# Output projection of a hybrid encoder step: prompt tokens in 2x2 blocks with seven products instead of eight

## The chip, the cores and the metric

The kernel runs on one core of one Trainium2 chip. The metric is device time in microseconds (us), from the start to the end of one execution, as a median of several runs. All data are float32. TensorE is called PE, VectorE DVE, ScalarE ACT, GpSimd POOL, and SyncE, which only issues transfers here, SP.

## The reference, cut to what matters

One layer of an encoder trunk is computed for 512 prompt tokens and 8 x 16 sample tokens (640 in all), with D_MODEL = 2048. Three gated attention branches are merged, and one output projection with an RMS norm and a residual follows. Only the last line is touched by the change:

```python
merged = (sigmoid(mg_sb) * branch(o_sb, g_sb, w_up_sb)
          + sigmoid(mg_bd) * branch(o_bd, g_bd, w_up_band)
          + sigmoid(mg_mm) * branch(o_mm, g_mm, w_up_mem))
return x + rms_norm(merged @ w_out, g_post)      # (640, 2048) @ (2048, 2048)
```

## The kernel before, in words

Float32 products are made of three matmuls. Every operand is split into a high part (a cast on ACT, `split`, L119) and a low part (the difference to the high part, on DVE, L120), and `mm3` (L175 to L178) adds high x high, high x low and low x high in a PSUM bank. The two parts of a weight tile are called `wh` and `wl`, those of `merged` `gh` and `gl`.

The instructions' order on each engine is fixed when the program is built; a scheduler that simulates the program places each instruction, and each engine then runs its own list in order and waits at the semaphores of its operands. What stands in a list before a waiting instruction's successor therefore counts.

Most of the span is the input projection. It already works on 2x2 blocks with seven products (`block_pair`, L746 to L808): POOL adds and subtracts weight blocks (L753, L800), ACT and DVE split the results, PE multiplies (L760). Then come attention heads with the rest of the gates between them, and the up projections (`up_steps`, L895): for each of the 16 blocks of 128 channels j, PE fills `acc`, DVE multiplies with the gate (L909), POOL adds into `merged[:, j]` (L910).

The output projection (L947 to L1029) is the part that the change replaces. `merged` has channels on the partitions, in 16 blocks of 128 (index k), and 640 tokens along a row. All 16 blocks are split when they are ready. Then four column blocks `cb` of 512 output columns follow one another, each with five PSUM banks `ya`, one for 128 tokens: for k in steps of two, SP loads a weight slab of 512 KB (`wr`, a ring of three buffers), ACT and DVE split it into `wh` and `wl` (rings of four), and PE runs 5 x 2 x 3 = 30 matmuls of 512 columns. At the end of a column block ACT takes the sums of squares (`square`, L986) and DVE scales by the gain into `yt` (`scale`, L989).

In the last column block the second half of k is kept in four slabs of their own, and the token blocks are finished one by one (4, 0, 1, 2, 3): 24 matmuls, `scale`, `square`, a chain of small operations for the norm's factor (L1019 to L1023), four multiply-adds with the residual `xres` (L1025), and the stores. So the last PE work of a token block lies under the closing work of the one before.

Of the kernel before, what the change touches and what calls it, by code (L numbers as in the profile page):

```python
# [32 lines left out]


B = dict(wr=3, wh=4, wl=4, kc=2, kt=4, vc=8, b=2, e=2, raw=1, q=1, k=1, v=1, wt=1)
LATE = 4

BESIDE = 24
PACE = 8
FIRST = 4  # L40
# [8 lines left out]
def stream_step_kernel(  # L49
# [57 lines left out]
    def rows_of(prompt, sample, t):  # L107
        return prompt[t * P:(t + 1) * P] if t < 4 else sample
# [9 lines left out]
    def split(hi, lo, src):  # L118
        ACT.copy(hi, src)  # L119
        DVE.tensor_tensor(lo, src, hi.bitcast(F32), op=ALU.subtract)  # L120
# [54 lines left out]
    def mm3(out, ah, al, bh, bl, start, stop):  # L175
        PE.matmul(out, ah, bh, start=start, stop=False)  # L176
        PE.matmul(out, ah, bl, start=False, stop=False)  # L177
        PE.matmul(out, al, bh, start=False, stop=stop)  # L178
# [687 lines left out]
    def fill_steps(done):  # L866
        for i in gates[-BESIDE:]:
            yield from gate_steps(i)

        xs.close()  # L870
        pm = br.enter_context(tc.tile_pool(name="mraw", bufs=1, side="right", reuse_waits="tile"))
# [94 lines left out]
    yt = [py.tile([P, D], F32, name=f"yt{t}") for t in range(5)]  # L966
    ssq = py.tile([P, 5, 4], F32, name="ssq")
    part = py.tile([P, 5], F32, name="part")
    for cb in range(4):
        cs = slice(cb * 512, (cb + 1) * 512)  # L970
        accs = [ps_y.tile([P, 512], F32, tag="ya", name="ya") for _ in range(5)]

        def w_slab(k0, *where):
            return load_w(w_o[k0 * P:(k0 + 2) * P, cs].rearrange("(k p) c -> p k c", p=P), [P, 2, 512], *where)

        def mm(t, k0, wh, wl):
            c = slice(t * P, (t + 1) * P)
            for kk in range(2):
                k = k0 + kk
                gh, gl = (g[:, c] for g in gparts[k])  # L980
                mm3(accs[t], gh, gl, wh[:, kk], wl[:, kk], k == 0, k == KB - 1)

        def square(t):

            sq = py.tile([P, 512], F32, tag="sq2", name="sq2", bufs=1)
            ACT.activation(sq, accs[t], AF.Square, scale=D ** -0.5, accum_out=ssq[:, t, cb:cb + 1])  # L986

        def scale(t):
            DVE.tensor_tensor(yt[t][:, cs], accs[t], gpb[:, cs], op=ALU.mult)  # L989

        late = 0 if cb < 3 else LATE
# [4 lines left out]
        if not late:  # L996
            for t in range(5):
                square(t)
                scale(t)
            continue  # L1000
        early.close()
        px = ctx.enter_context(tc.tile_pool(name="px", bufs=1, reuse_waits="tile"))
        slabs = [(k0, *w_slab(k0, py, 2 * LATE)) for k0 in range(KB - 2 * late, KB, 2)]
        xres = []
        for t in (4, 0, 1, 2, 3):
            x = px.tile([P, D], F32, name=f"xres{t}")
            SP.dma_start(x, rows_of(x_p, x_s, t))
            xres.append(x)
            DVE.tensor_reduce(part[:, t:t + 1], ssq[:, t, 0:3], op=ALU.add, axis=AX.X)
            DVE.tensor_scalar(part[:, t:t + 1], part[:, t:t + 1], EPS, None, op0=ALU.add)  # L1010
        for t, x in zip((4, 0, 1, 2, 3), xres):
            for sl in slabs:
                mm(t, *sl)
            scale(t)
            square(t)

            n = py.tile([P, 4], F32, tag="n", name="n", bufs=2)
            v, s_, r, q = (n[:, i:i + 1] for i in range(4))
            DVE.tensor_tensor(v, ssq[:, t, 3:4], part[:, t:t + 1], op=ALU.add)  # L1019
            ACT.activation(s_, v, AF.Sqrt)  # L1020
            DVE.reciprocal(r, s_)
            DVE.scalar_tensor_tensor(q, r, r, v, op0=ALU.mult, op1=ALU.mult)
            DVE.scalar_tensor_tensor(q, q, -3.0, r, op0=ALU.add, op1=ALU.mult)  # L1023
            for c in (slice(n * 512, (n + 1) * 512) for n in range(4)):
                DVE.scalar_tensor_tensor(yt[t][:, c], yt[t][:, c], q, x[:, c], op0=ALU.mult, op1=ALU.add)  # L1025
# [30 lines left out]
```

## Time and profile before

| what | value |
|---|---|
| time, median of 3 runs | 2049.0 us (2047.3 to 2050.6) |
| profiled execution: span from first to last instruction | 2044.4 us |
| what the median has beyond that span | 4.6 us |
| PE busy | 2014.2 us, 99% |
| DVE, ACT, POOL busy | 1178.5, 839.1, 705.8 us |
| chain that ended last | PE 91%, DMA 3%, DVE 2% |
| output projection | from 1816.9 us to the end |

The span belongs to one profiled execution; times of runs are a few us longer than a span because they hold what lies around it. In a row of a group, the numbers behind the bar are the total busy time in us, the mean time of one instruction in ns, and the idle time of its engine just before, with what ended it. In a row of the timeline the first two numbers are the start and the length in us. The records of PE show a matmul longer than the distance to the next one, since matmuls are pipelined.

### The profile page before, as it was taken

The page shows a single profiled execution, that of the slowest core. Times are in us where ns is not written, and L with a number is a line of the kernel's source. Part 1 is how long each engine was busy: PE and PEld are TensorE (multiplying, and loading weights), DVE is VectorE, ACT ScalarE, POOL GpSimd, SP SyncE. Part 2 cuts the span into 40 slices and gives each one's busy share as a digit, 9 for nine tenths or more (in the row PEclk, how much of TensorE's full clock was granted, in tenths as well). Part 3 has the DMA queues.
Part 4 walks back from the last instruction along what each step waited for, and adds up shares of the span by engine and source line. Part 5 has one row for each costly group of instructions (what it writes and reads, how often), then busy time and mean ns, then how long its engine had stood idle before and what let it go on. Part 6 is the DMA issues. An engine that isn't in the chain of part 4 may idle for free.

```text
span 2044.4 us, 35948 instructions
## 1 busy us (share of the span) xinstructions
PE 2014.2 (99%) x13829; PEld 1908.3 (93%) x13829; DVE 1178.5 (58%) x1830; ACT 839.1 (41%) x1577; POOL 705.8 (35%) x685
## 2 busy tenths in 40 slices
PE   8999999999999999999999999999999999999998
PEld 5999999999999999999998899999998899998886
DVE  6875577655676655555555555555556675442234
ACT  6544444444444444444443444444444332322221
POOL 1145566665666665644431011011010024330000
PEclk9999999999999999999999999999999999999999
DMA  7656676665686564663338777677679876532225
GB/s 269 218 140 150 169 207 142 168 168 149 161 205 154 137 156 130 150 150 111 118 106 280 224 221 219 214 225 225 211 214 283 255 234 178 144 123 83 73 93 216
DMA packets 548185, 361.38 MB, mean 177 GB/s; under 512 B 249169, under 2 KB 493409, under 8 KB 546477
## 3 DMA queue, kind: packets, MB, share of 16 engines
q1 hardware_dynamic: 528414, 305.80, 53.5%
q0 software_dynamic: 12688, 37.57, 5.5%
q10 hardware_dynamic: 6912, 15.73, 2.1%
q8 instruction: 108, 1.77, 0.4%
q14 instruction: 63, 0.52, 0.1%
HBM read 303.17 MB, written 90.77 MB: 193 GB/s over the span
## 4 chain that ended last, share of the span: by engine, by line
PE 91%; DMA 3%; DVE 2%; issue 1%; ACT 1%; POOL 1%; SPq 0%; ACTq 0%; DVEq 0%; POOLq 0%
PE q L760 44%; PE acc L191 27%; PE ya L176 4%; PE ya L178 4%; PE ya L177 4%; PE s L549 2%; PE o L608 1%; DMA or<-osg_d 1%; DVE wl L120 1%; PE tp L451 1%; PE acc L178 1%; PE acc L176 1%; PE acc L177 1%; PE o L177 1%; PE o L178 0%
## 5 line engine op out<-in xcount | busy, mean ns | idle before, releaser
L120 DVE TENSOR_TENSOR wl<-wr,wh 128x512 fp32r<-128x512 f32 (+1 forms) x516 | 411.7, 803 | 301.0 <-ACT wh L119 298.0
L119 ACT CAST wh<-wr 128x512 fp32r<-128x512 f32 (+1 forms) x516 | 311.7, 608 | 564.3 <-PE q L760 214.8
L120 DVE TENSOR_TENSOR wl<-ws,wh 128x512 fp32r<-128x512 f32 x304 | 285.1, 943 | 235.8 <-ACT wh L119 230.0
L760 PE MATMUL q<-xh,wl 128*128 128x320 f32 x1216 | 375.8, 309 | 0.3 <-DVE wl L120 0.3
L760 PE MATMUL q<-xh,wh 128*128 128x320 f32 x1216 | 375.7, 309 | 0.0
L760 PE MATMUL q<-xl,wh 128*128 128x320 f32 x1216 | 375.6, 309 | 0.0
L119 ACT CAST wh<-ws 128x512 fp32r<-128x512 f32 x304 | 188.1, 621 | 291.4 <-PE q L760 236.6
L760 PE MATMUL q<-th,wh 128*128 128x320 f32 x912 | 282.2, 309 | 2.0 <-ACT sig L777 2.0
L760 PE MATMUL q<-th,wl 128*128 128x320 f32 x912 | 281.9, 309 | 0.0
L760 PE MATMUL q<-tl,wh 128*128 128x320 f32 x912 | 281.8, 309 | 0.0
L760 PEld LDWEIGHTS q<-xh,wl 128*128 128x128 f32 x1216 | 228.7, 188 | 0.5 <-DVE wl L120 0.5
L760 PEld LDWEIGHTS q<-xl,wh 128*128 128x128 f32 x1216 | 228.6, 188 | 0.0
L760 PEld LDWEIGHTS q<-xh,wh 128*128 128x128 f32 x1216 | 228.5, 188 | 0.0
L191 PE MATMUL acc<-xh,wh 128*128 128x320 f32 x896 | 210.8, 313 | 0.0
L191 PE MATMUL acc<-xl,wh 128*128 128x320 f32 x896 | 209.5, 311 | 0.0
L191 PE MATMUL acc<-xh,wl 128*128 128x320 f32 x896 | 207.4, 310 | 0.0
L753 POOL TENSOR_TENSOR ws<-wr 128x512 f32<-128x512 f32 x114 | 169.1, 1496 | 81.2 <-DVE wl L120 68.5
L760 PEld LDWEIGHTS q<-th,wh 128*128 128x128 f32 x912 | 171.2, 188 | 2.7 <-ACT sig L777 2.5
L760 PEld LDWEIGHTS q<-th,wl 128*128 128x128 f32 x912 | 171.2, 188 | 0.2 <-DVE wl L120 0.2
L760 PEld LDWEIGHTS q<-tl,wh 128*128 128x128 f32 x912 | 171.2, 188 | 0.0
L191 PEld LDWEIGHTS acc<-xh,wh 128*128 128x128 f32 x896 | 150.1, 188 | 18.9 <-issue 18.4
L191 PEld LDWEIGHTS acc<-xl,wh 128*128 128x128 f32 x896 | 151.2, 188 | 0.6 <-issue 0.4
(228 smaller groups left out, 3353.1 us busy)
## 6 DMA issues: line engine op xcount, KB each, us to landing
wr<-in_w_in_dram SPq DMA_DIRECT2D x208, 512.0 KB, 4.9
kc<-keys_d SPq DMA_DIRECT2D x48, 512.0 KB, 5.8
wr<-in_w_out_dram SPq DMA_DIRECT2D x32, 512.0 KB, 3.7
sig_d<-sig ACTq DMA_DIRECT2D x48, 320.0 KB, 5.1
sig<-sig_d SPq DMA_DIRECT2D x48, 320.0 KB, 3.6
keys_d<-in_cache_sb_k_dram SPq DMA_DIRECT2D x96, 128.0 KB, 4.7
keys_d<-in_cache_band_k_dram SPq DMA_DIRECT2D x96, 128.0 KB, 4.5
vc<-in_cache_sb_v_dram SPq DMA_DIRECT2D x48, 256.0 KB, 5.6
```

The costliest lines, as they stand in the source:

```text
L119: ACT.copy(hi, src)
L120: DVE.tensor_tensor(lo, src, hi.bitcast(F32), op=ALU.subtract)
L176: PE.matmul(out, ah, bh, start=start, stop=False)
L177: PE.matmul(out, ah, bl, start=False, stop=False)
L178: PE.matmul(out, al, bh, start=False, stop=stop)
L191: PE.matmul(acc[:, s, :HF], a[:, k], b[s], start=first and f, stop=last and l)
L451: PE.transpose(tp[:, kb * P:(kb + 1) * P], b[:, kb * P:(kb + 1) * P], ident)
L549: return PE.matmul(s[32 * j:32 * j + 32, :nc_], qm[:, j, par * 32:par * 32 + 32], kts[j], start=par == 0, stop=par == 1, tile_position=(0, ...
L608: PE.matmul(o[32 * j:32 * j + 32, :P], l, r, start=i == 0, stop=i == len(steps) - 1, tile_position=(0, 32 * j))
L753: eng.tensor_tensor(o, a[c], b[c], op=op)
L760: PE.matmul(bank_, a[:, k], b[:, k], start=first and k == 0 and n == 0, stop=k == KH - 1 and n == 2, skip_group_check=not first)
```

## The change

The 512 prompt tokens are cut into two halves of 256, the 2048 inner channels k into two halves of 8 blocks, and the 2048 output columns into four parts of 512: g = 0, 1 each with a left and a right part. For each g the prompt part is a 2x2 block product, and it is computed with seven block products in place of eight. A11 to A22 are the quarters of `merged` (first index the half of the tokens, second the half of k), W11 to W22 those of the weights of one g. With S = A21+A22 and T = S-A11 the row operands are A11, S, T, A12, A12-T, A22-T and A22; with U = W12-W11 and V = W22-U the weight operands that they meet are W11, U, V, W21, W22, W22-W12 and W21-V. The 128 sample tokens are not blocked: they are multiplied plainly by four of the weight operands (W11, U, W21, W22), which is enough since the product with W11 is used for the left and the right part.

The work runs product by product, each for both g. In the text the stages are counted thus:

| stage | row operand, weight operand | matmuls |
|---|---|---|
| 1 | g1 = A11, W11; samples too | 144 |
| 2 | g5 = S, `tw` = U; samples too | 144 |
| 3 | g6 = T, `tw` = V | 96 |
| 4 | g2 = A12, W21; samples too | 144 |
| 5 | g3 = A12-T, W22, samples too (18 matmuls a step), and g7 = A22-T, W22-W12 (12 a step) | 240 |
| 6 | g4 = A22, `tw` = W21-V | 96 |

There are 864 matmuls of 512 columns in place of 960, and 112 weight tiles of 128x512 to be split in place of 64. The differences of weights are formed on POOL in tiles of 128x1024 (32 of them; L1047, L1064, L1097, L1115 of the changed kernel), two of the operands need two loaded slabs, and the loads of `w_out` are 48 of 512 KB in place of 32. Row operands live in two buffers that are used in turn, so each can be split only when the one two before it is done. Of the eight PSUM banks four (`ya`) hold sums over several products, two (`cc`) a product for a pair of token blocks, two (`cs`) the samples'. Finished parts are added into `yt` by DVE (L1028), squared by ACT and scaled by the gain on POOL (L1021). The residual is loaded into the place of `merged`. The up projection's blocks are made in the order 0, 8, 1, 9, ... so that the sums of the quarters can be formed early; otherwise everything ahead of the output projection stands in the same order as before on every engine.

The diff, cut to its core:

```diff
-    for j in range(KB):
-        split(*gparts[j], merged[:, j])
...
-    for cb in range(4):
-        cs = slice(cb * 512, (cb + 1) * 512)
-        accs = [ps_y.tile([P, 512], F32, tag="ya", name="ya") for _ in range(5)]
...
-        for k0 in range(0, KB - 2 * late, 2):
-            wh, wl = w_slab(k0)
-            for t in range(5):
-                mm(t, k0, wh, wl)
...
+    for g in range(2):
...
+        for k in range(0, KH, 2):
+            r = slab(0, g, 0, k)
+            with tc.issue_after(behind):
+                SP.dma_start(tw[g][:, k:k + 2], w_at(0, g, 1, k))
+            p = cut(r)
+            POOL.tensor_tensor(tw[g][:, k:k + 2], tw[g][:, k:k + 2], r, op=ALU.subtract)
+            for i in range(2):
+                times(ya[g][i], g1h, g1l, tok[i], k, p, True, True)
+            times(s, sh, sl, everything, k, p, True, True)
...
+    g7 = rows(a11)
+    for g in range(2):
+        s, cc = one_bank(), pair_banks()
+
+        def third(k):
+            r = slab(1, g, 1, k)
+            q = slab(0, g, 1, k)
+            p = cut(r)
+            POOL.tensor_tensor(q, r, q, op=ALU.subtract)
+            times(s, sh, sl, everything, KH + k, p, True, True)
+            for i in range(2):
+                times(cc[i], *g3, tok[i], k, p, True, True)
+            return q
+
+        q = third(0)
+        for k in range(0, KH, 2):
+            p = cut(q)
+            if k + 2 < KH:
+                q = third(k + 2)
+            into(g, *g7, k, p)
+        for i in range(2):
+            add(i, at(g, 1), cc[i])
+        add(4, at(g, 1), s)
+        for i in range(2):
+            add(2 + i, at(g, 1), ya[g][i])
+        for i in (0, 1, 4, 2, 3):
+            done_at(i, at(g, 1))
...
+    g4 = rows(a22)
...
+    for k in range(0, KH, 2):
+        into(0, *g4, k, cut(tw[0][:, k:k + 2]))
+    for i in range(2):
+        square(2 + i, at(0, 0), ya[0][i])
+        scale(2 + i, at(0, 0), ya[0][i])
...
+    slabs = [(k, cut(tw[1][:, k:k + 2], *((pl, 4) if k >= 4 else ()))) for k in range(0, KH, 2)]
+    for t in (4, 0, 1):
+        finish(t)
+    for i in range(2):
+        for k, p in slabs:
+            into(1, *g4, k, p, (i,))
+        scale(2 + i, at(1, 0), ya[1][i])
+        square(2 + i, at(1, 0), ya[1][i])
+        finish(2 + i)
```

`slab` loads 512 KB into the ring `wr` (three buffers as before), `cut` splits two tiles of 128x512 into `wh` and `wl`, `rows` splits a row operand in four tiles of 128x512, `times` and `into` issue the matmuls of one step of two k, and `finish` is the chain of the norm with the four multiply-adds and the stores.

Where the instructions stand. First DVE at the end. Before, each of the last token blocks has this list to itself (`yt_20765` and `yt_20766` are token blocks 2 and 3):

```order
L989 TENSOR_TENSOR yt_20765<-ya,gpb 128x512
L1019 TENSOR_TENSOR n<-ssq,part 128x1
L1021 RECIPROCAL n<-n 128x1
L1022 SCALAR_TENSOR_TENSOR n<-n 128x1
L1023 SCALAR_TENSOR_TENSOR n<-n 128x1
L1025 SCALAR_TENSOR_TENSOR yt_20765<-yt_20765,n,xres_22011 128x512 x4
L989 TENSOR_TENSOR yt_20766<-ya,gpb 128x512
```

Now the beginning of stage 6 reads thus on DVE (`yt_20801`, `yt_20797` to `yt_20800` are token blocks 4 and 0 to 3; `ya_20806` and `ya_20807` are the banks of g = 1):

```order
L118 TENSOR_TENSOR wl<-tw,wh 128x512
L1028 TENSOR_TENSOR yt_20801<-cs,yt_20801 128x512
L1028 TENSOR_TENSOR yt_20797<-cc,yt_20797 128x512
L1028 TENSOR_TENSOR yt_20798<-cc,yt_20798 128x512
L118 TENSOR_TENSOR gl<-merged,gh 128x512 x4
L1028 TENSOR_TENSOR yt_20799<-ya_20806,yt_20799 128x512
L118 TENSOR_TENSOR wl<-tw,wh 128x512
L1028 TENSOR_TENSOR yt_20800<-ya_20807,yt_20800 128x512
```

Between the first and the second weight tile of the stage stand four adds of stage 5's results and the four tiles of the row operand. Further down, in the middle of stage 6, DVE has:

```order
L1149 SCALAR_TENSOR_TENSOR yt_20797<-yt_20797,n,merged 128x512 x4
L1139 TENSOR_TENSOR n<-ssq,part 128x1
L118 TENSOR_TENSOR wl<-tw,wh 128x512 x7
L1141 RECIPROCAL n<-n 128x1
L1021 TENSOR_TENSOR yt_20799<-ya_20804,gpb 128x512
L1156 TENSOR_TENSOR part<-ssq 128x1
L1021 TENSOR_TENSOR yt_20800<-ya_20805,gpb 128x512
L1156 TENSOR_TENSOR part<-ssq 128x1
L1142 SCALAR_TENSOR_TENSOR n<-n 128x1
L118 TENSOR_TENSOR wl<-tw,wh 128x512
```

The four multiply-adds of token block 0 have moved ahead of the last eight weight tiles, and the last tile of all (the second k of the second step) stands behind two scalings.

On POOL the whole output projection had one instruction (the last additions into `merged` stand ahead of it, the store of the samples behind it):

```order
L910 TENSOR_TENSOR merged<-merged,sig 128x640 x21
L965 TENSOR_SCALAR gpb<-gpb 128x2048
L1029 DMA out_dram<-yt_20767 128x2048
```

Now it has, from stage 5's third to its eighth and last difference of weights:

```order
L1115 TENSOR_TENSOR wr<-wr 128x1024 x3
L1021 TENSOR_TENSOR yt_20797<-yt_20797,gpb 128x512
L1021 TENSOR_TENSOR yt_20798<-yt_20798,gpb 128x512
L1021 TENSOR_TENSOR yt_20801<-yt_20801,gpb 128x512
L1021 TENSOR_TENSOR yt_20799<-yt_20799,gpb 128x512
L1115 TENSOR_TENSOR wr<-wr 128x1024
L1021 TENSOR_TENSOR yt_20800<-yt_20800,gpb 128x512
L1115 TENSOR_TENSOR wr<-wr 128x1024 x2
```

Four scalings of finished results stand between the fifth and the sixth of the stage's eight differences, and a fifth scaling between the sixth and the last two.

More of the change, by code (lines that the diff above doesn't have):

```diff
@@ L35 @@
 B = dict(wr=3, wh=4, wl=4, kc=2, kt=4, vc=8, b=2, e=2, raw=1, q=1, k=1, v=1, wt=1)
-LATE = 4
 BESIDE = 24
@@ new lines, in w_at, with slab, cut, at @@
+    def w_at(half, g, right, k):
+        c = (2 * g + right) * C
+        r = (half * KH + k) * P
+        return w_o[r:r + 2 * P, c:c + C].rearrange("(k p) c -> p k c", p=P)
+    def slab(half, g, right, k):
+        t = pw.tile([P, 2, C], F32, tag="wr", name="wr", bufs=B["wr"])
+        SP.dma_start(t, w_at(half, g, right, k))
+        return t
+    def cut(t, *where):
+        return parts_of([t[:, n:n + 1] for n in range(2)], *where)
+    def at(g, right):
+        return slice((2 * g + right) * C, (2 * g + right + 1) * C)
@@ new lines, in times, with square @@
+    def times(acc, gh, gl, c, k0, parts, first, last):
+        wh, wl = parts
+        for n in range(2):
+            k = k0 + n
+            mm3(acc, gh[:, k, c], gl[:, k, c], wh[:, n], wl[:, n], first and k % KH == 0, last and k % KH == KH - 1)
+    tok = [slice(i * P, (i + 1) * P) for i in range(2)]
+    everything = slice(0, P)
+    def square(t, cs, src):
+        sq = stg.tile([P, NT], F32, tag="sig", name="sq")
+        n = cs.start // C
+        ACT.activation(sq[:, :C], src, AF.Square, scale=D ** -0.5, accum_out=ssq[:, t, n:n + 1])
@@ new lines, in scale, with done_at, add, pair_banks @@
+    def scale(t, cs, src, eng=DVE):
+        eng.tensor_tensor(yt[t][:, cs], src, gpb[:, cs], op=ALU.mult)
+    def done_at(t, cs, eng=POOL):
+        square(t, cs, yt[t][:, cs])
+        scale(t, cs, yt[t][:, cs], eng)
+    def add(t, cs, src, other=None):
+        DVE.tensor_tensor(yt[t][:, cs], src, yt[t][:, cs] if other is None else other, op=ALU.add)
+    ya = [[ps_y.tile([P, C], F32, name=f"ya{g}{i}") for i in range(2)] for g in range(2)]
+    def pair_banks():
+        return [ps_y.tile([P, C], F32, tag="cc", name="cc", bufs=2) for _ in range(2)]
@@ new lines, in one_bank @@
+    def one_bank():
+        return ps_y.tile([P, C], F32, tag="cs", name="cs", bufs=2)
+    for g in range(2):
+        cs1, cs2 = at(g, 0), at(g, 1)
+        s = one_bank()
+        for k in range(0, KH, 2):
[8 more added lines that the diff above has]
+        for i in range(2):
+            ACT.copy(yt[i][:, cs1], ya[g][i])
+        for c in (cs1, cs2):
+            ACT.copy(yt[4][:, c], s)
@@ new lines, in stream_step_kernel @@
+    rowsum(a21, a21, a11, ALU.subtract)
+    g6 = rows(a21)
+    for g in range(2):
+        cs1, cs2 = at(g, 0), at(g, 1)
+        s, cc = one_bank(), pair_banks()
+        for k in range(0, KH, 2):
+            p = cut(tw[g][:, k:k + 2])
+            r = slab(1, g, 1, k)
+            POOL.tensor_tensor(tw[g][:, k:k + 2], r, tw[g][:, k:k + 2], op=ALU.subtract)
+            times(s, sh, sl, everything, k, p, True, True)
+            for i in range(2):
+                times(cc[i], g5h, g5l, tok[i], k, p, True, True)
+        for i in range(2):
+            ACT.copy(yt[2 + i][:, cs2], cc[i])
+        add(4, cs2, s)
@@ new lines, in into @@
+    def into(g, gh, gl, k, p, which=(0, 1)):
+        wh, wl = p
+        for i in which:
+            for n in range(2):
+                a, b = gh[:, k + n, tok[i]], gl[:, k + n, tok[i]]
+                for l, r in ((a, wh), (a, wl), (b, wh)):
+                    PE.matmul(ya[g][i], l, r[:, n], start=False, stop=k + n == KH - 1 and r is wh and l is b,
+                              skip_group_check=True)
+    for g in range(2):
+        for k in range(0, KH, 2):
+            into(g, *g6, k, cut(tw[g][:, k:k + 2]))
+        for i in range(2):
+            add(i, at(g, 1), ya[g][i], yt[2 + i][:, at(g, 1)])
@@ new lines, in stream_step_kernel @@
+    g2 = rows(a12)
+    rowsum(a11, a22, a21, ALU.subtract)
+    rowsum(a21, a12, a21, ALU.subtract)
+    g3 = rows(a21)
+    for g in range(2):
+        s, cc = one_bank(), pair_banks()
+        for k in range(0, KH, 2):
+            r = slab(1, g, 0, k)
+            p = cut(r)
+            POOL.tensor_tensor(tw[g][:, k:k + 2], r, tw[g][:, k:k + 2], op=ALU.subtract)
+            times(s, sh, sl, everything, KH + k, p, True, True)
+            for i in range(2):
+                times(cc[i], *g2, tok[i], k, p, True, True)
+        for i in range(2):
+            add(i, at(g, 0), cc[i])
+        add(4, at(g, 0), s)
+        for i in (0, 1, 4):
+            done_at(i, at(g, 0))
```

123 lines of the change are left out of this document (67 added, 56 removed).

## Prediction

> **What bounds the kernel now.** I read the page's busy times and its chain first, then the busy times by stretches, then the groups of the output projection.
>
> ```profile
> span 2044.4 us, 35948 instructions
> PE 2014.2 (99%) x13829; PEld 1908.3 (93%) x13829; DVE 1178.5 (58%) x1830; ACT 839.1 (41%) x1577; POOL 705.8 (35%) x685
> PE 91%; DMA 3%; DVE 2%; issue 1%; ACT 1%; POOL 1%; SPq 0%; ACTq 0%; DVEq 0%; POOLq 0%
> 500.00:600.00 100.00, 100.00 (x683) 99.91 (x682) 65.38 (x75) 40.18 (x74) 63.96 (x64) 1.00 0.72 184
> 1850.00:2000.00 150.00, 150.00 (x663) 124.24 (x662) 45.72 (x77) 41.36 (x82) 0.00 (x0) 1.00 0.27 90
> 1816.00:2036.00 220.00, 218.58 (x960) 180.11 (x960) 13.61 (x20) 13.06 (x38) 1.00 0.33 114
> ```
>
> The last three rows are stretches: length, then busy time and count on PE, weight load, DVE, ACT and POOL, granted clock, DMA share. PE never rests: neither in a stretch of the input projection, which already works with seven products (POOL 64% and DVE 65% busy beside it), nor in the output projection, where DVE and ACT are below a third and POOL does nothing. So a matmul less counts in full, as long as the other engines keep up. The third stretch holds the 960 matmuls into `ya` alone: 218.58 / 960 = 0.2277 us each.
>
> **The change part by part.** 960 - 864 = 96 matmuls go: 96 x 0.2277 = 21.9 us off the path. That the change does not do this is excluded by its list of instructions. Everything else is a question of cover. The prices:
>
> ```profile
> L120 DVE TENSOR_TENSOR wl<-wr,wh 128x512 fp32r<-128x512 f32 x62 | 41.9, 691 | 119.3 <-ACT wh L119 119.3
> L119 ACT CAST wh<-wr 128x512 fp32r<-128x512 f32 x62 | 37.8, 622 | 124.2 <-PE ya L178 111.2 <-DMA wr<-in_w_out_dram 11.0 <-PE acc L191 0.9
> L986 ACT ACTIVATE sq<-ya 128x512 f32<-128x512 f32 x20 | 12.0, 599 | 40.3 <-DVE yt L989 31.5 <-PE ya L178 8.4
> L986 ACT ACTIVATION_READ_ACCUMULATOR sq<-ya 128x1 f32 x20 | 3.9, 194 | 0.0
> L965 POOL TENSOR_SCALAR gpb<-gpb 128x2048 f32<-128x2048 f32 x1 | 5.4, 5404 | 7.3 <-issue 7.3
> wr<-in_w_out_dram SPq DMA_DIRECT2D x32, 512.0 KB, 3.7
> wr<-in_w_in_dram SPq DMA_DIRECT2D x208, 512.0 KB, 4.9
> 511.71 1.28 POOL L800 TENSOR_TENSOR ws<-wr,ws 128x512 f32<-128x512 f32 x1 [0.63 <-DVE wl L120]
> 516.27 1.75 POOL L753 TENSOR_TENSOR ws<-wr,wr 128x512 f32<-128x512 f32 x1
> 522.35 3.00 POOL L753 TENSOR_TENSOR ws<-wr 128x512 f32<-128x512 f32 x2 [0.63 <-DVE wl L120]
> 523.05 1.14 DVE L120 TENSOR_TENSOR wl<-wr,wh 128x512 fp32r<-128x512 f32 x1 [0.78 <-ACT wh L119]
> 524.31 0.49 DVE L770 TENSOR_TENSOR sig<-sig,q 128x320 f32<-128x320 f32 x1
> 526.57 0.69 DVE L120 TENSOR_TENSOR wl<-wr,wh 128x512 fp32r<-128x512 f32 x1 [0.67 <-ACT wh L119]
> 527.83 0.49 DVE L770 TENSOR_TENSOR sig<-sig,q 128x320 f32<-128x320 f32 x1 [0.56 <-PE q L760]
> ```
>
> A low part costs DVE 0.69 us with POOL at rest, and 1.14 beside a running POOL operation; POOL's 128x512 costs 1.28 to 1.75. A 128x1024 difference is not in this trace: I take twice a 128x512 one, 2.6 to 3.5 us, and 2.7 where DVE has little to do. A DVE operation that reads PSUM (L770) takes 0.49 beside POOL and without it, so the adds from PSUM are not slowed.
>
> *Stages 1 to 4 (528 matmuls).* Stage 1's weights pass a ring of three slabs, and a slab is now freed only when POOL has subtracted it. POOL's last addition into `merged` comes first:
>
> ```profile
> 1816.88 0.40 PE L176 MATMUL ya<-wh,gh 128*128 128x512 f32 x1
> 1818.03 1.89 POOL L910 TENSOR_TENSOR merged<-merged,sig 128x640 f32<-128x640 f32 x1 [3.39 <-issue]
> ```
>
> From 1819.9: three differences (8.1), the gain's scaling (5.4), a fourth difference (2.7) end at 1836.1; the load into the freed slab (3.7), cast and low part (1.3) make the seventh slab ready at 1841.1. PE wants it after six steps of 18 matmuls (4.1 us each), at 1841.5: just in time, and 2.8 us later with 3.4 a difference (4 x 0.7), so 2.4 late. At the starts of stages 2, 3 and 4 the four tiles of the next row operand and two or three adds stand on DVE between two weight tiles: 6 or 7 x 0.69 = 4.1 to 4.8 us, under 12 to 18 matmuls (2.7 to 4.1 us) and the tiles that are split ahead. I take 1.0 us for all four, 0 to 3.
>
> *Stage 5 (240).* A step has 30 matmuls, 6.83 us, and needs two slabs of the ring of three. The slab that is to become W22-W12 can only be loaded when POOL's last difference has freed its place, so a step is at least one load, one difference and the hand-overs: 3.7 + 2.7 + 0.3 = 6.7 us, or with 3.5 a difference 7.5. (The hand-over is the idle time in the ACT row of the next fence, 0.23, rounded up.) Eight steps: 0 to 8 x 0.7 = 5.4 us. In the second half four scalings (4 x 1.3 = 5.2 us) stand on POOL between two differences; of these the chain can absorb most, since the slab behind them is still being loaded. I take 2.5.
>
> *Stage 6 (96) and the end.*
>
> ```profile
> 2029.90 0.69 DVE L989 TENSOR_TENSOR yt<-ya,gpb 128x512 f32<-128x512 f32 x1
> 2032.48 2.74 DVE L1025 SCALAR_TENSOR_TENSOR yt<-yt,n,xres 128x512 f32<-128x512 f32 x4
> 2034.59 0.40 PE L176 MATMUL ya<-wh,gh 128*128 128x512 f32 x1
> 2034.83 0.39 PE L177 MATMUL ya<-wl,gh 128*128 128x512 f32 x1
> 2035.06 0.40 PE L178 MATMUL ya<-wh,gl 128*128 128x512 f32 x1
> 2035.50 0.69 DVE L989 TENSOR_TENSOR yt<-ya,gpb 128x512 f32<-128x512 f32 x1 [0.28 <-PE ya L178]
> L1020 ACT ACT_TABLE_LOAD x1 | 1.3, 1283 | 0.0
> 2037.19 0.20 ACT L1020 ACTIVATE n<-n 128x1 f32<-128x1 f32 x1 [0.23 <-DVE n L1019]
> ```
>
> Before, closing a token block takes 5.3 us of DVE's list (2029.90 to 2035.22), under the 24 matmuls (5.5 us) of the next; after the last block's start at 2035.50 the span has 8.9 us left. Now count from the moment when PE has done stage 5. DVE has just ended that stage's last low parts (1.8 before, since they waited for POOL's last difference). Then its list has ten operations up to the second weight tile: 10 x 0.69 = 6.9, so this tile is there at 5.1. PE can run 8 matmuls without it; the first step ends at 5.1 + 4 x 0.23 = 6.0 in place of 2.7. The next two tiles stand behind an add and three small operations (0.2 each) and come at 7.0 and 7.7; step 2 ends at 9.4, step 3 at 12.1. For step 4 ACT is late: block 2 is added at 4.4, block 3 at 5.8, and behind them ACT has two squares (0.79 each, to 6.9), a cast, a table load, two roots and a cast (0.6 + 1.3 + 0.4 + 0.6 = 2.9), so the tiles of step 4 come at 10.5 and, behind three small operations, 11.8; it ends at 14.9, not 10.9. Then the four multiply-adds of block 0 (2.74) hold back g = 1: its first tile is there at 15.6, the next that PE wants is sixth in the list, at 15.6 + 5 x 0.69 = 19.1, and the last stands behind one more, two scalings and four or five small operations, at 22.6. From there 28 matmuls remain: PE ends at 22.6 + 6.4 = 29.0 in place of 21.9, 7.1 us late. The last two blocks have only their 14 last matmuls apart (3.2 us), less than the 5.3 of a closing: block 1's four multiply-adds fill DVE until 25.8, block 2's closing runs from there to 31.1, and only then block 3's begins, 1.9 after its matmuls; the span ends at 31.1 + 8.9 = 40.0, against 21.9 + 0.4 + 8.9 = 31.2 without any wait. So stage 6 and the end cost 8.8 us. POOL runs five scalings and four residual additions here, 9 x 1.3 = 11.7 us, and a DVE operation beside one loses up to 1.14 - 0.69 = 0.45: on some ten of them 0 to 5 us; I take 3.0.
>
> Row operands and their sums (32 tiles), 22 adds and 48 more weight tiles (102 x 0.69 = 70 us on DVE, and some 50 on ACT) lie beside 197 us of matmuls elsewhere and cost nothing there; if they stuck, PE would show idle time in the middle of a stage. Loads rise from 16 to 24 MB at a DMA share of 0.27: nothing, but for the ring.
>
> Sum: -21.9 + 1.0 + 2.5 + 8.8 + 3.0 = -6.6 us, a span of 2037.8. The median of the runs lies 4.6 above the profiled span (2049.0 - 2044.4), so 2042.4 us.
>
> **A rule that speaks against the change.** POOL and DVE now run beside each other through the whole section. The rows show a shared, not a blocked, path: the pair of POOL operations from 522.35 took 1.50 each, and the low part that began at 523.05 ended at 524.19, while waiting for the end of the first and then running would have given 522.35 + 1.50 + 0.69 = 524.54. By the Trainium skill, "SBUF — State Buffer", section "Who interferes with whom", a DVE operation with two SBUF inputs and a GpSimd operation that reads SBUF take a shared port in turn, and the loser is blocked for the whole instruction. The trace does not agree with the whole instruction; it agrees that an operand from PSUM goes free.
>
> **The rivals.**
> - *Hidden.* The waits of stage 6 overlap better than my list, as the block products of the input projection do at 100% PE. Against it: there DVE has no row operands, adds and closings in its list. Only the end's 1.8 and some 2 us remain: -21.9 + 3.8 = -18.1, 2030.9 us. Chance 0.13.
> - *Eaten.* All terms near their upper ends: +3 +5.4 +8.8 +5 = 22.2 against 21.9; 2045 to 2053, at 2049.3. Chance 0.27.
> - *Slower: the ring of three slabs in stage 5.* With a load as in the input projection (4.9), a difference of twice 1.75 and the hand-over, a step lasts 8.7 us, 1.9 over its matmuls; 8 steps cost 15: -21.9 + 1 + 15 + 8.8 + 3 = +5.9, 2054.9 us. It decides from 8.5 us a step on (about +4); for it speaks that 2 MB of the residual are loaded in the middle of this stage, against it the 3.7 in this very section. Chance 0.07.
> - *Slower: each POOL operation blocks DVE for its whole length.* In stage 5, POOL's 8 x 2.7 + 8 x 1.3 = 32.0 us, DVE's 36 low parts (24.8) and 8 adds (5.5) then exclude each other: 62.3 us against 54.6, +7.7; in stage 6 the 11.7 us count in full: -21.9 + 1 + 7.7 + 8.8 + 11.7 = +7.3, 2056.3 us. Chance 0.05; this is the rule of that page, which the rows above do not bear out.
>
> **How the numbers follow.** The forecast, a gain of some 4 to 13 us, has the remaining 0.48. 0.2% (4.1 us) is about what a measurement of this kernel can tell from no change. Faster: 0.48 + 0.13 = 0.61; same: 0.27; slower: 0.07 + 0.05 = 0.12. The range runs from the hidden case, 2031, into the eaten one, 2051, which leaves out both slower cases and a half of the hidden one, some 0.19. The likeliest case's own range is 2036 to 2045.
>
> **What would show it.** Right: 864 matmuls into the `ya`, `cc` and `cs` banks at 0.23 us, PE without idle time in stages 1 to 4 but for a few tenths; in stage 5 idle time in front of the matmuls on W22-W12, released by DVE or ACT whose own wait is for POOL (L1115) or for `wr`; in stage 6 about 7 us of idle PE, released by DVE's `wl` (L118), and the last block's scaling about 2 us after its last matmul. Wrong: idle time of several us at the starts of stages 2 to 4, a low part of 2 us and more beside POOL, or a matmul interval other than 0.2277 (it is 0.233 between the last rows of the section, where one bank takes 24 in a row; 864 x 0.006 would be 5 us), or a first matmul of the section later than 1816.9 since the up projection's lists have changed too.

## The result, and the profile after

The changed kernel takes 2058.1 us (median of four runs, 2054.1 to 2059.3) against 2049.0 before: 1.0042 of the time, 95% interval 1.0028 to 1.0055. Measured again beside other kernels on another occasion it took 2053.6 against 2048.1, 1.0030 (1.0020 to 1.0040). So it is slower by 0.3 to 0.4%, where a gain of 0.3% was forecast, and 96 matmuls less have made the kernel longer.

First the page of the changed kernel: span, busy times, the chain that ended last.

```profile
span 2055.3 us, 36123 instructions
PE 2003.1 (97%) x13733; PEld 1895.3 (92%) x13733; DVE 1294.3 (63%) x1936; ACT 882.9 (43%) x1677; POOL 821.8 (40%) x737
PE 88%; DVE 4%; DMA 3%; issue 2%; POOL 1%; ACT 1%; SPq 0%; DVEq 0%; ACTq 0%; POOLq 0%
```

PE was idle for 30.2 us of the span before (2044.4 - 2014.2) and is for 52.2 now; DVE has gone from 2% of the chain to 4%, and POOL is busy 116 us longer. The output projection in stretches, in the columns of the prediction's stretches:

```profile
1820.00:1840.00 20.00, 12.98 (x51) 10.07 (x50) 17.93 (x11) 3.51 (x7) 18.45 (x7) 0.87 0.57 214
1840.00:1930.00 90.00, 89.64 (x392) 73.66 (x392) 69.16 (x72) 41.90 (x73) 43.07 (x17) 0.99 0.32 103
1930.00:1960.00 30.00, 27.53 (x122) 22.38 (x121) 27.74 (x23) 14.48 (x31) 22.82 (x11) 1.00 0.46 147
1960.00:2012.00 52.00, 50.03 (x213) 40.64 (x212) 34.23 (x43) 21.13 (x42) 24.24 (x13) 0.97 0.42 134
2012.00:2055.30 43.30, 25.62 (x96) 18.60 (x94) 35.88 (x66) 17.33 (x42) 15.43 (x10) 0.86 0.51 194
```

The loss has three places: the first 20 us (stage 1), the start and the middle of stage 5 (which runs from 1950.6 to 2011.8), and stage 6. The 90 us of the second stretch are full. What happens in the first place is seen on DVE, POOL and PE beside each other:

```profile
1823.47 2.60 DVE L977 TENSOR_TENSOR merged<-merged 128x256 f32<-128x256 f32 x1 [1.45 <-POOL merged L908]
1825.99 2.49 DVE L118 TENSOR_TENSOR sl<-merged,sh 128x128 fp32r<-128x128 f32 x1
1828.40 2.58 DVE L118 TENSOR_TENSOR gl<-merged,gh 128x256 fp32r<-128x256 f32 x1
1831.02 4.74 DVE L971 TENSOR_TENSOR merged<-merged 128x512 f32<-128x512 f32 x2
1835.68 7.59 DVE L118 TENSOR_TENSOR wl<-wr,wh 128x512 fp32r<-128x512 f32 x5
1823.39 7.31 POOL L1047 TENSOR_TENSOR tw<-tw,wr 128x1024 f32<-128x1024 f32 x3
1830.68 5.54 POOL L984 TENSOR_SCALAR gpb<-gpb 128x2048 f32<-128x2048 f32 x1
1836.42 0.79 PE L175 MATMUL ya<-wl,gh 128*128 128x512 f32 x1 [7.02 <-DVE wl L118]
1837.01 0.63 PE L176 MATMUL ya<-wh,gl 128*128 128x512 f32 x1
1837.43 0.63 PE L174 MATMUL ya<-wh,gh 128*128 128x512 f32 x1
```

Five operations of DVE, of 128x128 to 128x512, take 12.4 us; without POOL beside them they last 0.28, 0.43 and 0.69 by their sizes (so a little earlier in the same trace, at 1818.6 to 1819.4), some 2.5 together. Each of the first three lasts about as long as one of POOL's differences (7.31 / 3 = 2.44); of the next two, the first takes 4.02 beside the gain's scaling and the second its usual 0.69. The trace counts that as busy time of DVE, not as a wait, so no view of waits names POOL. Behind them stand the weight tiles, and PE stands still for 7 us; then its matmuls start 0.43 us apart in place of 0.2277 for some 4 us.

To compare runs I use the section from the first matmul into a `ya` bank to the end. That first matmul came at 1816.9 in the profile before, at 1820.4 here, and anywhere from 1815.2 to 1823.2 in the runs below. It moves with the lists unchanged: a second profile of the changed kernel has it at 1817.2, and the probe below, which has the lists of before on PE, DVE and ACT, at 1820.9. Why, no run shows; so differences of some 4 us between two times need not come from the output projection. The section was 227.5 us before and is 234.9 now, 7.4 more; without any wait it would be 21.9 less. It repeats better than the times: 234.9 and 233.8 in the two profiles of the changed kernel. All other kernels were profiled once.

### The profile page after: what moved, and what is told of

The parts are those of the page before. It is cut to its first block, busy times and chain, and to the rows that moved or that the text cites. A ratio compares the mean times of both kernels' runs of the same rounds, so it can differ in the third digit from the quotient of the medians.

```text
span 2055.3 us, 36123 instructions
## 1 busy us (share of the span) xinstructions
PE 2003.1 (97%) x13733; PEld 1895.3 (92%) x13733; DVE 1294.3 (63%) x1936; ACT 882.9 (43%) x1677; POOL 821.8 (40%) x737
## 4 chain that ended last, share of the span: by engine, by line
PE 88%; DVE 4%; DMA 3%; issue 2%; POOL 1%; ACT 1%; SPq 0%; DVEq 0%; ACTq 0%; POOLq 0%
PE q L758 46%; PE acc L189 28%; DVE wl L118 2%; PE s L547 2%; PE o L606 1%; PE ya L1079 1%; DMA or<-osg_d 1%; DMA wr<-in_w_out_dram 1%; PE cc L174 1%; PE cc L175 1%; PE cc L176 1%; PE tp L449 1%; POOL merged L908 1%; DVE yt L1149 1%; PE cs L175 1%
## 5 line engine op out<-in xcount | busy, mean ns | idle before, releaser
L118 DVE TENSOR_TENSOR wl<-wr,wh 128x512 fp32r<-128x512 f32 (+1 forms) x516 | 440.8, 863 | 220.5 <-ACT wh L117 216.3
L117 ACT CAST wh<-ws 128x512 fp32r<-128x512 f32 x304 | 188.1, 621 | 287.7 <-PE q L758 232.4
L758 PEld LDWEIGHTS q<-xh,wh 128*128 128x128 f32 x1216 | 228.5, 188 | 0.0
L798 POOL TENSOR_TENSOR ws<-wr,ws 128x512 f32<-128x512 f32 x76 | 99.9, 1315 | 146.8 <-DVE wl L118 143.7
```

The source lines that it names most:

```text
L758: PE.matmul(bank_, a[:, k], b[:, k], start=first and k == 0 and n == 0, stop=k == KH - 1 and n == 2, skip_group_check=not first)
L798: POOL.tensor_tensor(b, a, b, op=ALU.subtract)
```

## The experiments

All runs in one table. "Stages 1 to 5, lost" is the time from the section's first matmul to the start of stage 6 beyond 768 x 0.2277 us; stage 6 starts with the 96th matmul from the end, and the last matmul is taken to end 0.2277 us after its start. The length of a hole is given in the text from matmul start to matmul start, less 0.2277 us; the idle time in the rows of PE is some 0.16 shorter. The ratio is to the kernel before on the same chip; the runs were made on several chips, so ratios are compared and not medians.

| kernel | median us | ratio (95%) | section | stages 1 to 5, lost | stage 6 to the end | of it behind the last matmul |
|---|---|---|---|---|---|---|
| before | 2049.0 | | 227.5 | | | 9.1 |
| p1: before, with work on POOL | 2051.2 (one run) | | 228.5 | | | 9.1 |
| the change | 2058.1 | 1.0042 (1.0028 to 1.0055) | 234.9 | 16.5 | 43.5 | 11.1 |
| after_again: the same | 2053.6 | 1.0030 (1.0020 to 1.0040) | 233.8 | 16.3 | 42.6 | 11.1 |
| e1: differences in halves | 2050.0 | 1.0009 (0.9997 to 1.0021) | 231.4 | 9.3 | 47.2 | 11.2 |
| e2: differences on DVE | 2048.4 | 1.0002 (0.9992 to 1.0011) | 228.5 | 8.9 | 44.7 | 11.1 |
| e3: nothing on POOL | 2042.8 | 0.9966 (0.9956 to 0.9977) | 222.3 | 4.4 | 43.0 | 11.2 |
| e4: e3, closings later | 2036.3 | 0.9952 (0.9940 to 0.9964) | 218.0 | 5.2 | 38.0 | 13.8 |
| e5: e4, residual later | 2034.6 | 0.9945 (0.9933 to 0.9958) | 213.1 | 0.3 | 38.0 | 13.8 |
| e6: the change, closings later | 2052.9 | 1.0027 (1.0015 to 1.0039) | 232.4 | 16.7 | 40.8 | 15.6 |
| e7: e5, scalings later | 2034.7 | 0.9942 (0.9929 to 0.9954) | 213.2 | 0.1 | 38.2 | 14.5 |
| e8: gain's scaling on ACT | 2057.6 | 1.0049 (1.0035 to 1.0063) | 232.7 | 15.1 | 42.7 | 11.1 |
| e9: e8, short differences | 2039.3 | 0.9959 (0.9945 to 0.9972) | 220.9 | 3.5 | 42.6 | 11.1 |

The scheduler moves some instructions when a length or an engine changes, so only the probe, e8 and after_again have the very lists on PE and DVE of the kernel that they are compared with; in the others DVE's order differs in places.

**p1_probe: what does a POOL operation cost DVE?** The kernel before, with this added:

```diff
+    idle = py.tile([P, D], F32, name="idle")
+    POOL.memset(idle, 1.0)
+    for w, n in ((1024, 16), (512, 24), (2048, 8), (256, 40)):
+        for _ in range(n):
+            POOL.tensor_tensor(idle[:, :w], idle[:, :w], idle[:, :w], op=ALU.mult)
```

> The kernel before, with POOL multiplying a dead tile by itself at the start of its output projection: 16 times 128x1024, 24 times 128x512, 8 times 128x2048, 40 times 128x256. The lists of the other engines stay as they are. Theory A (a POOL operation holds DVE off until it ends): a low part of DVE, 0.69 us alone, lasts up to about the length of the POOL operation that it meets, so up to 2.4 us beside 128x1024, 1.3 beside 128x512, 4.8 to 5 beside 128x2048, about 0.9 beside 128x256; the scaling from PSUM stays at 0.69. Theory B (the two share the path evenly, so that a DVE operation is slowed by a factor): a low part lasts 1.1 to 1.4 us beside every size. The total: no change by either, 2049, unless 128x2048 makes DVE late.

Four stretches of its output projection, each beside one size on POOL; count, then shortest, median and longest in ns, then first and last start:

```profile
L973 POOL TENSOR_TENSOR idle<-idle x35: 614/615/1122, 1935.1 to 1962.0; 128x256 f32<-128x256 f32 x35
L120 DVE TENSOR_TENSOR wl<-wr,wh x8: 692/1065/1133, 1937.7 to 1958.9; 128x512 fp32r<-128x512 f32 x8
L973 POOL TENSOR_TENSOR idle<-idle x11: 1042/1042/1370, 1885.5 to 1897.6; 128x512 f32<-128x512 f32 x11
L120 DVE TENSOR_TENSOR wl<-wr,wh x4: 750/1407/1522, 1889.1 to 1896.6; 128x512 fp32r<-128x512 f32 x4
L973 POOL TENSOR_TENSOR idle<-idle x12: 1895/2222/2449, 1837.2 to 1861.9; 128x1024 f32<-128x1024 f32 x12
L120 DVE TENSOR_TENSOR wl<-wr,wh x8: 692/1501/2311, 1841.5 to 1862.6; 128x512 fp32r<-128x512 f32 x8
L973 POOL TENSOR_TENSOR idle<-idle x7: 3928/3929/4094, 1902.8 to 1927.0; 128x2048 f32<-128x2048 f32 x7
L120 DVE TENSOR_TENSOR wl<-wr,wh x7: 1905/4083/4087, 1903.4 to 1927.4; 128x512 fp32r<-128x512 f32 x7
L994 DVE TENSOR_TENSOR yt<-ya,gpb x5: 676/692/693, 1870.9 to 1876.7; 128x512 f32<-128x512 f32 x5
```

The same low part of 0.69 us lasts up to 1.13, 1.52, 2.31 and 4.09 us: it grows with the POOL operation, to that operation's length and 0.2 to 0.5 more, and beside 128x2048 more than half of them last a whole POOL operation (median 4083). Even sharing (theory B) is out. POOL's own operations grow by up to 0.55, most of one DVE operation; so the two engines seem to take turns, one of yours, one of mine, and the rows of stage 1 above and of e8 below show it one operation at a time. The scaling with an operand in PSUM (L994, beside the 128x512 operations) stays at 0.69. The time of the probe, 2051.2 us in its one run, lies within what the kernel before took on that chip (2044.5 to 2054.9).

**e1_half: shorter operations on POOL.**

```diff
+    def diff(out, a, b):
+        for n in range(2):
+            POOL.tensor_tensor(out[:, n:n + 1], a[:, n:n + 1], b[:, n:n + 1], op=ALU.subtract)
...
-            POOL.tensor_tensor(tw[g][:, k:k + 2], tw[g][:, k:k + 2], r, op=ALU.subtract)
+            diff(tw[g][:, k:k + 2], tw[g][:, k:k + 2], r)
```

(The other three differences in the same way.)

> The changed kernel with each of POOL's 32 weight differences in two operations of 128x512 in place of one of 128x1024. Theory A (blocked for one whole POOL operation): DVE's operations beside them last up to 1.3 us, not 2.5; the 7.2 us hole in stage 1 falls to 3 or 4 (the gain's scaling of 5.5 us on POOL stays), the sum of PE's holes from 26.5 to about 15, and the time from 2058 to about 2048. Theory B (shared evenly, the order of the lists makes the holes): DVE's operations and the holes stay, 2055 to 2061.

The time speaks for theory A, and in stage 1 a hole of 3.6 us is left, as it said, with one of 1.5 behind it. The holes in sum shrank less than it said (to 23.0 us): stages 1 to 5 lose 9.3 in place of 16.5, but stage 6 takes 4 more, with another order of DVE's list there.

**e2_dve and e3_nopool: the work moved to DVE.** e2 has `DVE.tensor_tensor` in the four places; e3 also

```diff
-    POOL.tensor_scalar(gpb, gpb, -0.5, None, op0=ALU.mult)
+    ACT.mul(gpb, gpb, -0.5)
-    def done_at(t, cs, eng=POOL):
+    def done_at(t, cs, eng=DVE):
```

and the samples' residual by the same multiply-adds as the other token blocks.

> The changed kernel with the 32 weight differences on DVE in place of POOL; the scaling of the gain and of the results stays on POOL. Theory A: a difference costs DVE about 1.4 us (twice a low part) in place of 2.4 us of being blocked, so the holes shrink to those of the gain's scaling in stage 1 (about 4 us) and of stage 6: 2043 to 2050. Theory B: DVE's list grows by 32 x 1.4 = 45 us and nothing else falls away: weight tiles come later in stages 1 and 5, 2060 or more.

> The changed kernel with nothing on POOL in the output projection: weight differences, scalings of results and the residual additions of the samples on DVE, the gain's scaling on ACT. Theory A: no DVE operation above 1.5 us; the hole of stage 1 is gone, the holes of stages 4 and 5 too, and what is left is the order of DVE's list in stage 6, about 7 us, and the end, 2 us: 2039 to 2046. Theory B: DVE carries 32 x 1.4 + 20 x 0.69 = 59 us more and comes late more often: 2060 or more.

Both times are as theory A says, e3's by 0.34% under the kernel before. In stage 1 the hole is 2.2 us in e2 and gone in e3. In stage 5 theory A missed: e2 still loses 6.8 us there, as much as the change, and e3 4.7; e5 below comes back to that. DVE does more and is busy for less. Low parts of the output projection in the changed kernel (first two rows) and in e3 (next two), then one group of differences and the busy times of e3:

```profile
L118 DVE TENSOR_TENSOR wl<-wr,wh 128x512 fp32r<-128x512 f32 x62 | 68.6, 1146 | 29.4 <-ACT wh L117 29.3
L118 DVE TENSOR_TENSOR wl<-tw,wh 128x512 fp32r<-128x512 f32 x48 | 48.4, 1049 | 9.3 <-ACT wh L117 9.2
...
L118 DVE TENSOR_TENSOR wl<-wr,wh 128x512 fp32r<-128x512 f32 x62 | 41.1, 686 | 16.0 <-ACT wh L117 15.7
L118 DVE TENSOR_TENSOR wl<-tw,wh 128x512 fp32r<-128x512 f32 x48 | 31.8, 686 | 13.2 <-ACT wh L117 13.0
L1000 DVE TENSOR_TENSOR tw<-wr,tw 128x1024 f32<-128x1024 f32 x16 | 19.5, 1221 | 3.6 <-DMA wr<-in_w_out_dram 3.4
PE 2002.2 (98%) x13733; PEld 1896.1 (93%) x13733; DVE 1270.2 (62%) x1988; ACT 883.0 (43%) x1674; POOL 701.1 (34%) x684
```

A difference costs DVE 1.22 us. So e3 puts 32 x 1.22 + 20 x 0.68 = 52.6 us more on DVE, and its busy time falls from 1294.3 to 1270.2: by this account about 77 us of the former were time in which POOL held it.

**e4_fin and e6_after_fin: the order of DVE's list in stage 6.** On e3 and on the changed kernel:

```diff
+    with tc.issue_after(last_on(DVE)):
         for t in (4, 0, 1):
             finish(t)
```

which sets these closings behind the last weight tile in DVE's list.

> The kernel of e3 (nothing on POOL), with the closing of token blocks 4, 0 and 1 (two factors and twelve multiply-adds) set behind the last weight tile of stage 6 in DVE's list. Theory C (DVE's order makes the hole of stage 6): the hole of 4.9 us in front of g = 1, the 2.7 us of slower matmuls behind it and the 1.9 of the end go, 2.0 of the e3 run's stage 5 stays: 2033 to 2037 against 2042.8. Theory D (these tiles wait for buffers that PE itself frees, and the multiply-adds only fill the time): the hole stays, and the closings come later at the end: 2042 to 2047.

> The changed kernel with POOL's work as it is, and only the closings of blocks 4, 0 and 1 behind the last weight tile on DVE. Theory C: the hole of 4.35 us in stage 6 and the 3 us of slow matmuls behind it go, and 1 to 2 of the end: 2049 to 2052 against 2058. If POOL's holds make that hole rather than the order: 2055 to 2058.

The hole in e3 and what stood on DVE in front of it (the multiply-adds, L1149):

```profile
2013.32 1.41 DVE L1149 SCALAR_TENSOR_TENSOR yt<-yt,n,merged 128x512 f32<-128x512 f32 x2
2014.65 0.68 DVE L118 TENSOR_TENSOR wl<-tw,wh 128x512 fp32r<-128x512 f32 x1
2015.25 4.06 DVE L1149 SCALAR_TENSOR_TENSOR yt<-yt,n,merged 128x512 f32<-128x512 f32 x6
2019.23 2.49 DVE L118 TENSOR_TENSOR wl<-tw,wh 128x512 fp32r<-128x512 f32 x4
2021.17 0.80 PE L1082 MATMUL ya<-wl,gh 128*128 128x512 f32 x1 [4.75 <-DVE wl L118]
```

In both kernels this hole is gone, as theory C says, but only a part of it is gained: stage 6 takes 38.0 in place of 43.0 us in e4, 40.8 in place of 43 in e6, since the closings now stand at the end (13.8 and 15.6 us behind the last matmul, not 11.1). The 2036.3 us of e4 lie within C's 2033 to 2037, but partly thanks to the chip, on which the kernel before took 2046.4 and not 2048.6; by the ratios e4 is 0.14% (2.9 us) under e3, with intervals that overlap, so its gain rests on the sections. In e6 that leaves next to nothing, 1.0027 against 1.0042 and 1.0030, and C's 2049 to 2052 was missed. From the moment when the tiles are done DVE, not PE, bounds the end.

**e5_finres: the residual behind the last slab.** On e4, `with tc.issue_after(last_on(SP)):` around the five loads of the residual.

> As e4, and the five loads of the residual (5 MB) stand on SP's queue behind the last weight slab, not in the middle of stage 5. Theory E (a load of the residual makes the slab behind it land late, 8.9 us in e3 in place of 3.4): the hole of 1.96 us in stage 5 and the slow matmuls behind it (1.6) go, so 3 to 4 us less than e4. Theory F (the ring of three slabs is what limits the step): no change to e4 within 1 us; and if the residual now comes too late for the first closing, up to 4 us more.

The losses of stages 1 to 5 go from 5.2 to 0.3 us: theory E. In e3, the cast on ACT that PE's hole in stage 5 waited for, and that hole, were

```profile
1957.02 1.14 ACT L117 CAST wh<-wr 128x512 fp32r<-128x512 f32 x2 [6.92 <-DMA wr<-in_w_out_dram]
1957.68 0.50 PE L174 MATMUL cs<-wh,sh 128*128 128x512 f32 x1 [1.81 <-ACT wh L117]
DMA to landing us min/median/max: 3.4/4.2/8.9
...
DMA to landing us min/median/max: 3.4/4.1/5.2
```

behind a slab that landed after 8.9 us; the last row is e5's, where none takes more than 5.2. The ring of three slabs then keeps up. By the medians it is 1.6 us to e4, by the sections 5.0, where theory E expected 3 to 4; the intervals of the two ratios overlap, so it is the rows that decide for E, not the time.

**e7_late: the last scalings behind the tiles.** On e5, `done_at` of stage 5's last results set behind the tiles of stage 6's first half.

> As e5, and the five scalings of stage 5's last results stand behind the weight tiles of stage 6's first half on DVE. Theory C: the second weight tile of stage 6 no longer waits for them, the holes of 0.4 and 1.7 us at the stage's start shrink below 1: 1 to 2 us less than e5, 2028 to 2033. If the four tiles of the row operand and the five adds make these holes instead: as e5.

No change in time, against theory C: stage 6 loses 1.8 in place of 2.3 us ahead of the last matmul, and the end takes 0.8 longer. That fits a DVE whose sum of work counts there and not its order.

**e8_gain, e9_short and after_again: one long operation, or all of them?** e8 is the changed kernel with `ACT.mul(gpb, gpb, -0.5)`; e9 has besides

```diff
+    def diff(out, a, b):
+        c = slice(0, C // 4)
+        POOL.tensor_tensor(out[:, :, c], a[:, :, c], b[:, :, c], op=ALU.subtract)
...
-            POOL.tensor_tensor(tw[g][:, k:k + 2], tw[g][:, k:k + 2], r, op=ALU.subtract)
+            diff(tw[g][:, k:k + 2], tw[g][:, k:k + 2], r)
```

(and so in the other three places; e9 leaves out three quarters of every difference).

> The changed kernel with the gain's scaling (128x2048, 5.5 us) on ACT in place of POOL; the lists of PE and DVE are the same word for word, POOL's differences close ranks. Theory A (each POOL operation holds DVE off): the hole of 7.2 us in stage 1 falls by the scaling's length to 1.5 to 3, and the slower matmuls behind it (2.3 us) with it: 5 to 7 us less than the changed kernel, 2050 to 2053. Theory G (the hole is made by the slab that a late difference frees): the difference behind the scaling is 5.5 us earlier too, so the hole goes in this case as well; they differ in DVE's operations, which by A still last 2.4 to 2.6 us each beside the differences, by G 0.7 to 1.1.

> As e8, and each of POOL's weight differences takes only the first quarter of its columns (128x256 in all); the rest of the weight operand stays raw, so this part of the computation is left out. The number of POOL's operations and DVE's work stay. Theory A: holds of about 0.7 us in place of 2.4, nothing above 0.5 us of a hole in stages 1 to 5, but the scalings and the residual additions still hold DVE in stage 6: 2045 to 2049. If the number of operations or the order of DVE's list counts and not their length: as e8.

> The changed kernel itself, beside e8 and e9 on one chip: 2055 to 2060, holes as in its first profile; the first matmul of the output projection anywhere from 1815 to 1822 us, since everything ahead of it stands in the same lists.

e8 missed: I expected 5 to 7 us less than the change and got none of it. Its median is even 4.0 us above after_again's, with a section 1.2 us shorter; its first matmul into `ya` came 6 us later (1823.2 and 1817.2), which is not explained. Its stage 1:

```profile
1826.24 2.60 DVE L977 TENSOR_TENSOR merged<-merged 128x256 f32<-128x256 f32 x1 [1.46 <-POOL merged L908]
1828.77 2.49 DVE L118 TENSOR_TENSOR sl<-merged,sh 128x128 fp32r<-128x128 f32 x1
1831.18 2.58 DVE L118 TENSOR_TENSOR gl<-merged,gh 128x256 fp32r<-128x256 f32 x1
1833.80 5.46 DVE L971 TENSOR_TENSOR merged<-merged 128x512 f32<-128x512 f32 x2
1839.18 2.48 DVE L118 TENSOR_TENSOR wl<-wr,wh 128x512 fp32r<-128x512 f32 x4
1826.17 12.54 POOL L1047 TENSOR_TENSOR tw<-tw,wr 128x1024 f32<-128x1024 f32 x5
1839.91 0.80 PE L175 MATMUL ya<-wl,gh 128*128 128x512 f32 x1 [7.74 <-DVE wl L118]
```

Where the scaling stood, two more differences have moved up, and the same five operations of DVE pass one by one behind five of POOL's. That rules theory G out too: DVE's operations last 2.5 to 2.7 us, and the tiles behind them, which POOL no longer meets, 0.62 (2.48 / 4). So the price is not the length of one POOL operation; it is the number of DVE operations in front of the awaited tile, times the POOL operation that each must let pass. e9 confirms it with the very list of e8 on DVE: with short differences on POOL the hole of stage 1 is gone, stages 1 to 5 lose 3.5 in place of 15.1 us, and the kernel takes 2039.3, below the 2045 to 2049 that I expected. One hole of 2.5 us stays at the start of stage 5, where I expected none above 0.5: the four `gl` tiles take 6.3 us there beside POOL's scalings. The change itself came out at 2053.6, a little under what I had put down for it; the holes are much as in its first profile.

## Why the prediction was wrong, point by point

The sum came to -6.6 us, and the section grew by 7.4. Of the 14 us between them nearly nine are missing in stage 1 and four in stage 5.

- *96 matmuls, -21.9: right.* In e5, where almost nothing holds PE, the section is 14.5 shorter than before, and what is missing to 21.9 is in sight: 4.7 more behind the last matmul, 2.3 lost in stage 6, 0.3 ahead of it.
- *Stages 1 to 4, +1.0 (0 to 3): the step that failed most.* Stage 1 alone lost 9.6 us (the hole of 7.2 and 2.4 by the slower matmuls behind it), stages 2 to 4 together 0.3. POOL's own queue ran about as reckoned: from the first difference to the end of the fourth 15.2 us, where 16.2 were forecast. Whether the seventh slab would have been in time was not tested, since PE was already late. Missing was that DVE's operations beside POOL's last as long as those: the forecast let stage 1's low parts take 0.69 us.
- *Stage 5, +2.5 (0 to 5.4).* It lost 6.5: a hole of 2.6 at its start, behind `gl` and `wl` beside POOL's differences and scalings, and one of 2.1 with slow matmuls (1.7) in its middle. The second also stands behind weight tiles that DVE made beside POOL's scalings, at some 1.8 us each for the first two:

```profile
1982.51 5.92 POOL L1021 TENSOR_TENSOR yt<-yt,gpb 128x512 f32<-128x512 f32 x4
1985.52 6.24 DVE L118 TENSOR_TENSOR wl<-wr,wh 128x512 fp32r<-128x512 f32 x3
1987.35 0.50 PE L1079 MATMUL ya<-wl,gh 128*128 128x512 f32 x1 [1.97 <-DVE wl L118]
```

  So the scalings, which the prediction had only as a delay of POOL's own chain, held DVE here. The load of the residual, which I had only as a rival, makes 4 to 5 us of losses in e3 and e4; in the changed kernel no slab landed later than 5.5 us (8.9 in e3), so it is not seen there, and it was not tried alone.
- *Stage 6 and the end, +8.8, and contention there, +3.0: right in size, the second term by luck.* 40.0 + 3.0 = 43.0 us were forecast from the end of stage 5 to the end; 43.5 and 42.6 were measured. Ahead of the last matmul PE has holes of 7.4 us in sum (7.1 forecast), and 2.0 us more than before lie behind it (1.9 forecast). The rest, 3.1 and 2.3 us in the two profiles, are slower matmuls behind the holes, which the sum did not have; that they are about as much as the contention put down is luck. e3, without POOL, takes 43.0 too, with five scalings and four multiply-adds (some 6 us) more on DVE; so whether POOL's holds lengthen this stage stays open. e4 and e6 show the cause of the largest hole (4.4 us) as the prediction had it, multiply-adds of finished blocks ahead of the tiles.
- *Contention priced at 0.45 an operation, in stage 6 only: the root.* It came from a row that stands for two operations, POOL's pair at 522.35 with 3.00 us, which I cut into 1.50 and 1.50. The two apart (shortest, median, longest), from the trace of before:

```profile
L753 POOL TENSOR_TENSOR ws<-wr x2: 1298/1520/1743, 522.3 to 523.6; 128x512 f32<-128x512 f32 x2
```

  The first ended at 523.65, not 523.85. The low part recorded from 523.05 to 524.19 ended 0.54 behind it, which is most of its own 0.69, as if it had waited for the end of the first. And the second took 1.74, 0.44 more than the first, as if it had waited in its turn. So these rows fit a block, and the probe shows it. The rule that I set aside, the Trainium skill's "SBUF — State Buffer", section "Who interferes with whom" (two SBUF inputs on DVE, a GpSimd operation that reads SBUF, one of them blocked for the whole instruction, an operand in PSUM free), is borne out by the probe: low parts last up to a whole POOL operation there, and the scaling from PSUM stays at 0.69. One POOL operation does not follow it: the gain's scaling held DVE for 3.74 of its 5.45 us in e2 (last section).
- *The rival "each POOL operation blocks DVE", 2056.3 at a chance of 0.05: the right mechanism, with the wrong places.* It put 7.7 us in stage 5 and 11.7 in stage 6 and nothing for it in stage 1, by adding up lengths; that its time came near the measured 2058.1 and 2053.6 is luck. What decides is where DVE's list is dense ahead of a tile that PE wants: stage 1.
- *The first matmul later than 1816.9:* it came later, but not because of the up projection's lists alone, if at all: the probe, with the unchanged lists of before, has it at 1820.93.

The other step, 4.6 us between span and time, held something that is no fixed cost: in every run that gives both, the time is 1.7 above the span (2057.0 to 2055.3 for the changed kernel). The remaining 2.9 mean that the one execution profiled before was a fast one; its early first matmul (1816.9) fits that.

## What to carry to other kernels

Before work is given to an idle POOL, count the DVE operations with two SBUF inputs that stand between PE and its next tile there: each had to let one POOL operation pass here, so long POOL operations are the expensive ones, and the same difference on DVE (1.22 us) was cheaper than being held by it (2.4). Look at DVE's mean length of the same operation before and after, because a hold is recorded as busy time, and take rows of several operations apart before reasoning on one of them. A hole that is closed by reordering gives its time back only as far as the engine behind it has slack: with POOL out of the way and residual and closings moved, the seven products gained 0.55% (0.9945, 0.9933 to 0.9958), and DVE's sum of work at the end kept the rest.

## What the runs showed of the hardware

- A small operation is held as well as a large one. In stage 1 a low part of 128x128, which takes 0.28 us alone, lasts 2.49; in stage 6 of the changed kernel two of three operations on 128x1 wait for POOL's scalings (1.6 us each, the second row): they take 0.64, 0.15 and 1.24 us, where 0.15 is usual.

```profile
2015.12 1.88 DVE L1157 SCALAR_TENSOR_TENSOR part<-part,ssq 128x1 f32<-128x1 f32 x3
2012.44 8.00 POOL L1021 TENSOR_TENSOR yt<-yt,gpb 128x512 f32<-128x512 f32 x5 [6.32 <-ACT sq L1018]
```

- The gain's scaling, which has one input tensor where POOL's other operations here have two, held DVE for a part of its length only. In e2, beside it (second row, to 1823.93), a 128x128 low part is held for 3.74 us, but the next low part and a difference then run at 0.41 and 1.21. In the changed kernel it held an addition for 4.02 of its 5.54 us. Whether the single input is the reason was not tested.

```profile
1818.60 3.74 DVE L118 TENSOR_TENSOR sl<-merged,sh 128x128 fp32r<-128x128 f32 x1
1818.48 5.45 POOL L984 TENSOR_SCALAR gpb<-gpb 128x2048 f32<-128x2048 f32 x1 [0.25 <-DMA gpb<-in_g_post_dram]
1822.26 0.41 DVE L118 TENSOR_TENSOR gl<-merged,gh 128x256 fp32r<-128x256 f32 x1
1822.60 1.21 DVE L1000 TENSOR_TENSOR tw<-tw,wr 128x1024 f32<-128x1024 f32 x1
```

- A hole on PE can cost more than its length: behind the 7 us of stage 1 matmuls start some 0.425 us apart for over 4 us, 2.4 us lost in all. The granted clock is 0.50 from 1837.0 to 1841.4 (0.87 is the mean of the stretch from 1820 to 1840). The Trainium skill, "TensorE: Matmul & The Clock Gate", section "Wait — 56ns, not 53.3ns?", has 426.7 ns for 512 columns on the slow clock; the trace agrees. The length of the hole alone does not decide: in e3 the hole of 1.97 us was followed by such matmuls (1959.00, 1959.42, 1959.85; clock 0.50), in e2 the one of 2.17 and in the changed kernel the one of 2.63 at 1959.12 were not (clock 1.00).
